# Hymba layer in fp32 on one core: the fold of the second down run, the spread of a row scale, and the Silu table are put elsewhere

## The chip, the cores and the metric

The kernel runs on one core of one Trainium2 chip. The metric is the device time of one execution in microseconds (us). Five engines work side by side: PE (TensorE, matrix products), DVE (VectorE), ACT (ScalarE), POOL (GpSimd) and SP (SyncE, which here only issues DMAs). Each runs its own instructions in order, and they wait for one another by semaphores.

## The reference

One encoder layer, T = 256 tokens, D = 2048, all in fp32. Each sub-layer is normed ahead and behind:

```python
x = x + 0.5 * rms_norm(swiglu(rms_norm(x, pre1), w_gate_up1, w_down1), post1)     # DFF = 5632
h = rms_norm(x, pre_m) @ w_in                                                     # HGRN2 and attention parts
x = x + rms_norm(concat(hgrn2(h), window_attention(h)) @ w_out, post_m)
x = x + 0.5 * rms_norm(swiglu(rms_norm(x, pre2), w_gate_up2, w_down2), post2)
def swiglu(x, w_gate_up, w_down):
    gate, up = split(x @ w_gate_up, 2)
    return (silu(gate) * up) @ w_down
```

The change touches both feed-forward networks (FFN1 and FFN2 below) and one step of the mixer between them.

## The kernel before

**Products.** Every fp32 operand is held as two f32r tiles: `split_act` (L175 to L177) rounds it on ACT (L176, "cast") and forms what is left on DVE (L177, "split"). One product of two such operands is three matmuls, high by high, high by low and low by high (`three`, L441 is the matmul). Weights arrive as `raw` tiles of 1 MB (two blocks of 128 rows by 1024 columns), and a pair of weight blocks is called a pair here.

**Gate and up.** The first stage of a network multiplies the tokens by the gate and up weights in groups of columns. While group 0 runs, the inputs `xt` are not yet normed; the row scale is put to use later. `spread` (L271 to L279) turns the two scale columns into a tile R that has one token's scale in each column: for each half m a tile `dg` is written by DVE as identity times scale (L277), a product with a tile of ones (L278) sums it over the partitions, and DVE copies the PSUM bank to R (L279). `dg` has one buffer, so the second half waits until PE has read the first. It is called in both networks and in the mixer. DVE then multiplies `xt` by R (`even`, L1045). The groups' results go through `units`: Silu of the gate on ACT with the scale as factor (L1075), the product with up on DVE (L1080), transposes on PE (L1100), a copy and a cast on ACT. For group 0 the scale is the norm's own.

**Down.** The second stage, class `Pairs`, goes over the hidden rows in 22 pairs (u = 0 to 21) twice, once for each half of the 2048 columns: the first and the second down run. A plain pair is 8 products (24 matmuls). The even pairs 0 to 18 are mixed pairs and use a scheme of 7 products (21 matmuls) in the manner of Strassen: the left sides are sums of hidden blocks, the right sides sums of weight blocks, and four of the seven go to side sums P1, P5, P6 and P7 that have PSUM banks of their own, beside the four result banks c00, c01, c10, c11. When the last mixed pair is done, `fold` spreads the side sums over the result banks: ACT copies P1 (L528), DVE forms three more sums (L529, L522, L523, L526), then adds one to each result bank (L535 for c00, L539, L543, L545). A result bank takes no product while its add is under way. In the second run, `play` runs the fold ahead of the pair that stands two places behind the last mixed one.

**What sets the order.** The table `orders` in `ffn` gives the pairs of the two runs; `steps` lists them; `added` names the mixed pairs one of whose block sums is formed by an accumulating DMA from POOL (`prepare`, L1234). The body of the runs is written in its order by hand (a manual schedule): at step i it splits pair i+1, prepares i+4, and multiplies pair i. `load_down` issues the next 1 MB load on SP (L1218) as soon as the last split has freed a buffer. The last two pairs of the second run, 20 and 21, are held: `finish` loads them by itself (L152), splits them, and multiplies bank by bank, so that each result bank is complete as early as possible. The splits of `finish` and the fold are put in one order by a scheduler.

Of the kernel before, what the change touches and what calls it, by code (L numbers as in the profile page):

```python
# [11 lines left out]
F32 = mybir.dt.float32  # L12
# [4 lines left out]
AF = mybir.ActivationFunctionType  # L17
# [3 lines left out]
P = 128  # L21
D = 2048
T = 256
# [14 lines left out]
def hymba_layer_kernel(  # L38
# [37 lines left out]
    def nm(s):  # L76
        uid[0] += 1
        return f"{s}_{uid[0]}"
# [76 lines left out]
    def split_load(src, hp=hip, lp=lop, between=None, middle=None):  # L155
        return split(load(src, between), hp, lp, middle)
# [83 lines left out]
    def pre_stats():  # L240
        with tc.issue_after(last["act"].ins):
            pre_stats_now()
# [29 lines left out]
    def spread(factor=rs2):  # L272

        ps = pb()
        for m in range(2):
            dg = stat.tile([P, P], F32, tag="dg", name=nm("dg"), bufs=1)
            nc.vector.tensor_scalar(dg, ident, factor[:, m : m + 1], None, ALU.mult)  # L277
            nc.tensor.matmul(ps[:, m * P : (m + 1) * P], ones, dg, start=True, stop=True)  # L278
        nc.vector.tensor_copy(R, ps[:, :T])  # L279


# [314 lines left out]
    class Pairs(Blocks):  # L596
# [3 lines left out]

        HELD = 2
        firsts = 2

        def __init__(self, w, orders, tiles, sums, room, gain_src, keep=(), near=()):

# [94 lines left out]
        def second_run(self):  # L700
# [3 lines left out]
                    self.gains(m, n)  # L704
            self.run(1)

        def finish(self, mul, post, new_x=None, gain=None, lead=None):


# [1 line left out]
            n_order = len(order)  # L711
            self.post = post
            self.work(n_order - self.HELD)
            held = []
            for u in order[n_order - self.HELD :]:
                held.append((u, *split_load(self.source(u), hp=post, lp=post)))
            close_far()
            self.half_gain(post)
            if new_x:
# [287 lines left out]
    def ffn(gated, w_dn, post_gain, again, gain=None, lead=None, aside=None):  # L1007

        with ExitStack() as st:
# [108 lines left out]
            def some(steps, n):  # L1118
                for _ in range(n):
                    next(steps)  # L1120

            pre_stats()
            last = KT // 2 - 1
            for u in range(gated.pos, KT // 2):
                gated.work(u + 1)
# [56 lines left out]
            def pair_ahead(g, u):  # L1182
# [16 lines left out]
            orders = [  # L1199
                [9, 11, 8, 13, 10, 15, 12, 1, 0, 3, 14, 5, 16, 17, 2, 7, 4, 19, 6, 18, 20, 21],  # L1200

                [2, 7, 4, 9, 6, 11, 8, 13, 10, 12, 15, 0, 5, 14, 3, 16, 1, 18, 17, 19, 20, 21],
            ]
            added = {0: (12, 0, 14, 16, 2, 4, 6, 18), 1: (2, 4, 6, 10, 12, 0, 14, 16, 18)}
            steps = [(r, u) for r in range(2) for u in orders[r]][: 2 * NU - Pairs.HELD]
            in_order = sorted(
                (i - 3.5 if u in added[r] else i, i) for i, (r, u) in enumerate(steps)
            )
# [29 lines left out]
                    )  # L1238

            def splits(i):  # L1240
                if i >= len(steps):
                    return
                r, u = steps[i]
                raw = raws[i]
# [38 lines left out]
            with tc.manual_schedule():  # L1283
# [34 lines left out]
                some(waiting, 1)  # L1318
                some(ahead, 1)
                products(1)  # L1320
                for i in range(2, len(steps)):
                    if i == NU + 18:
                        back_cm.__exit__(None, None, None)
                        early_cm.__exit__(None, None, None)
                        post = rows.post = st.enter_context(post_pool())
                    ahead = splits(i + 1)
                    next(ahead, None)
                    prepare(i + 4)
                    for u in fetch_at.get(i, ()):
                        fetch(u)  # L1330
                    next(ahead, None)
                    products(i)
                    for _ in ahead:
                        pass
                    if i in again_at:
                        sums[again_at[i]] = sums_again(again_at[i])
                    if i == 8:
                        rows.half_gain(far["pool"])
                    if i == NU - 1:
                        rows.second_run()  # L1340
            return rows.finish(
                mul=0.5, post=post, new_x=again, gain=gain and gain(), lead=lead
            )
# [625 lines left out]
```

## Time and profile before

| what | value |
|---|---|
| median of 3 runs | 1833.16 us (1832.65 to 1834.87) |
| the profiled execution | 1832.72 us |
| its span, first to last instruction | 1830.9 us |
| TensorE clock granted, mean | 0.998 |
| PE busy | 99% of the span |
| DVE, ACT, POOL busy | 87%, 62%, 8% |
| DMA | 444.45 MB, 243 GB/s on average |

The profile is of one execution. Its rows give the start in us from the beginning of the span, the duration, the engine, the line of the kernel, the operation, and the tile that is written with those that are read. A bracket at a row's end tells how long the engine stood idle ahead of it and whose result ended that. "x3" is a row of three like instructions with their time in all. Matmuls overlap, so their durations add up to more than the time; the distance between two starts is what one costs.

### The profile page before, as it was taken

What the parts mean: (1) busy time and instruction counts of PE and PEld (TensorE: products, weight loads), DVE (VectorE), ACT (ScalarE), POOL (GpSimd) and SP (SyncE); (2) the same over time, 40 slices, a digit from 0 to 9 for tenths busy, and PEclk for the clock granted to TensorE, in tenths of its full rate; (3) what the DMA queues carried; (4) which work ended last, traced back from release to release, by engine and by line L of the source; (5) the groups of instructions that cost most, each with busy time, mean ns of one, the idle gap of its engine ahead of it and who ended that gap; (6) DMA issues with size and microseconds to landing.
All of it is one profiled execution on the core that took longest, in us unless ns stands there. A gap on an engine that the chain in (4) does not pass through costs nothing.

```text
span 1830.9 us, 23436 instructions
## 1 busy us (share of the span) xinstructions
PE 1812.4 (99%) x8438; PEld 1503.5 (82%) x8438; DVE 1599.2 (87%) x2041; ACT 1130.9 (62%) x1496; POOL 155.5 (8%) x149
## 2 busy tenths in 40 slices
PE   9999999999999999999999999999999999999997
PEld 6888888888888887888888888788888888888886
DVE  7999999999989988477687798899999999998986
ACT  6565666665656666476587556556666666566663
POOL 1011111111011100000000000001111111011110
PEclk9999999999999999999999999999999999999999
DMA  8789999998698985555554456789999888699892
GB/s 301 230 231 289 275 280 255 252 262 242 231 341 267 301 263 192 187 191 165 169 166 150 170 210 245 218 244 266 282 273 270 255 245 253 199 345 290 272 328 106
DMA packets 210420, 444.45 MB, mean 243 GB/s; under 512 B 11656, under 2 KB 46560, under 8 KB 209536
## 3 DMA queue, kind: packets, MB, share of 16 engines
q1 hardware_dynamic: 180032, 385.14, 60.2%
q0 software_dynamic: 30272, 57.82, 18.2%
q8 instruction: 66, 1.08, 0.2%
q14 instruction: 50, 0.41, 0.1%
HBM read 430.31 MB, written 12.60 MB: 242 GB/s over the span
## 4 chain that ended last, share of the span: by engine, by line
PE 89%; DVE 4%; ACT 3%; DMA 2%; issue 2%; POOL 0%; SPq 0%; DVEq 0%; ACTq 0%; POOLq 0%
PE pa L441 39%; PE pb L441 33%; PE pa L309 5%; PE pa L314 3%; PE pa L364 2%; PE pa L363 2%; PE pa L362 2%; DVE l L177 2%; DMA raw<-in_w_ffn_gate_up_dram 2%; ACT h L176 1%; PE pa L1100 1%; PE pb L1100 1%; PE pb L1690 0%; PE pb L1664 0%; PE pb L1768 0%
## 5 line engine op out<-in xcount | busy, mean ns | idle before, releaser
L176 ACT CAST h<-raw 128x1024 fp32r<-128x1024 f32 (+1 forms) x861 | 851.0, 1013 | 467.6 <-PE pb L441 154.5
L177 DVE TENSOR_TENSOR l<-raw,h 128x1024 fp32r<-128x1024 f32 (+1 forms) x861 | 983.8, 1173 | 140.2 <-ACT h L176 106.0
L441 PE MATMUL pa<-h,xt 128*128 128x512 f32 x1104 | 387.9, 392 | 0.1
L441 PE MATMUL pb<-h,xt 128*128 128x512 f32 x952 | 340.7, 392 | 0.5 <-DVE pb L1152 0.4
L441 PEld LDWEIGHTS pa<-h,xt 128*128 128x128 f32 x1104 | 207.2, 188 | 44.2 <-DVE xt L232 0.6
L441 PE MATMUL pa<-l,xt 128*128 128x512 f32 x552 | 216.0, 391 | 0.1
L441 PEld LDWEIGHTS pb<-h,xt 128*128 128x128 f32 x952 | 178.7, 188 | 43.6 <-DVE pb L1159 3.9
L441 PE MATMUL pb<-l,xt 128*128 128x512 f32 x476 | 185.6, 390 | 0.0
L441 PE MATMUL pa<-h,ht 128*128 128x512 f32 x464 | 163.1, 390 | 3.8 <-DVE pa L535 3.8
L441 PE MATMUL pb<-h,ht 128*128 128x512 f32 x464 | 163.0, 390 | 0.0
L936 POOL DMA_DIRECT2D raw<-in_w_ffn_gate_up_dram x76 | 92.0, 1211 | 738.5 <-DVE l L177 647.0
L309 PE MATMUL pa<-xt,h 128*128 128x512 f32 x512 | 124.5, 393 | 0.2 <-ACT h L176 0.2
L441 PEld LDWEIGHTS pa<-l,xt 128*128 128x128 f32 x552 | 103.8, 188 | 21.5 <-DVE l L177 1.7
L309 PEld LDWEIGHTS pa<-xt,h 128*128 128x128 f32 x512 | 93.8, 188 | 18.6 <-ACT h L176 0.6
L441 PE MATMUL pa<-h,xs 128*128 128x512 f32 x304 | 108.9, 389 | 0.0
L441 PE MATMUL pb<-h,xs 128*128 128x512 f32 x304 | 106.0, 389 | 0.0
L441 PEld LDWEIGHTS pa<-h,ht 128*128 128x128 f32 x464 | 87.1, 188 | 22.6 <-issue 4.6
L441 PEld LDWEIGHTS pb<-l,xt 128*128 128x128 f32 x476 | 89.5, 188 | 17.0
L441 PEld LDWEIGHTS pb<-h,ht 128*128 128x128 f32 x464 | 87.1, 188 | 18.0
L441 PE MATMUL pa<-l,ht 128*128 128x512 f32 x232 | 90.4, 390 | 0.0
L441 PE MATMUL pb<-l,ht 128*128 128x512 f32 x232 | 90.3, 389 | 0.0
L1234 POOL DMA_DIRECT2D raw<-in_w_ffn_down_dram x34 | 41.2, 1211 | 366.2 <-DVE la L177 345.9
(287 smaller groups left out, 2550.8 us busy)
## 6 DMA issues: line engine op xcount, KB each, us to landing
raw<-in_w_ffn_gate_up_dram SPq DMA_DIRECT2D x350, 512.0 KB, 5.8
raw<-in_w_ffn_down_dram SPq DMA_DIRECT2D x88, 1024.0 KB, 7.9
raw<-in_w_mix_in_dram SPq DMA_DIRECT2D x52, 1024.0 KB, 4.9
raw<-in_w_ffn_gate_up_dram POOLq DMA_DIRECT2D x76, 512.0 KB, 8.4
raw<-in_w_ffn_down_dram POOLq DMA_DIRECT2D x34, 512.0 KB, 10.1
raw<-in_w_mix_out_dram SPq DMA_DIRECT2D x16, 1024.0 KB, 5.0
ht<-away SPq DMA_DIRECT2D x24, 512.0 KB, 10.5
away<-ht SPq DMA_DIRECT2D x16, 512.0 KB, 6.8
```

The lines of the kernel that those rows point to most:

```text
L176: nc.scalar.copy(hi, src)
L177: nc.vector.tensor_tensor(lo, src, hi.bitcast(F32), ALU.subtract)
L309: nc.tensor.matmul(slot[f], weights(hs, kk, f), xcol(xt, k), start=(k == 0), stop=(k == KT - 1))
L314: nc.tensor.matmul(slot[f][:, 0:T], weights(ls, kk, f), xcol(xt, kh * 8 + kk, 0), start=False, stop=False,)
L362: nc.tensor.matmul(dst, xh, h[:, o : o + n], start=(k == 0), stop=False)
L363: nc.tensor.matmul(dst, xh, l[:, o : o + n], start=False, stop=False)
L364: nc.tensor.matmul(dst, xl, h[:, o : o + n], start=False, stop=(k == KT - 1))
L441: nc.tensor.matmul(self.bank(at), lhs, rhs, start=(n == 1), stop=n in (ends, self.of[at]), skip_group_check=n > ends,)
L936: nc.gpsimd.dma_start(raw[:, 0:1024].rearrange("p (k c) -> p k c", k=2), self.source(u, g)[:, :, 1], accum_op=ALU.add,)
L1100: nc.tensor.transpose(bank[:, o : o + P], zs[m][:, k * P : (k + 1) * P], ident)
L1234: nc.gpsimd.dma_start(raws[i][:, 0:1024].rearrange("p (k c) -> p k c", k=2), Pairs.part(w_dn, u, r)[:, :, 512:1024], accum_op=ALU.add,)
```

## The change

It has three parts.

First, the second run's order is a new one in which mixed and plain pairs alternate strictly to the end; pair 18, mixed, stands at place 18 and pair 19 at place 19 (counted from 0). The held pairs are no longer loaded in `finish`: `steps` covers all 44, so `load_down` loads them in the common row, and `hold` splits them: pair 20 in step NU + 18, ahead of the products of pair 18, and pair 21 in the midst of the fold. The fold is written out behind the last pair of the loop: two parts (the sums and the add to c00), then pair 21's splits, then the other three adds.

Second, `spread` writes both halves of identity times scale into R itself, and one product of 256 columns takes the place of two of 128; the copy back to R stays. The tile `dg` is gone there; the helper `to_columns`, which used the same buffer, has it alone.

Third, behind `pre_stats()` in each network ACT is given one Silu of a 128 by 2 piece of a scratch tile.

The program is written anew around that. DVE at the end of FFN2's second run; `l` are splits (15343 and 15347 of pair 19, 15412 and 15416 of held pair 20, 15422 of held pair 21), `y` the fold's sums, `pa_14643` to `pb_14645` the result banks. Before:

```order
L177 TENSOR_TENSOR l_15343<-raw_10171,h_15342 128x1024
L177 TENSOR_TENSOR l_15412<-raw_15409,h_15411 128x1024
L177 TENSOR_TENSOR l_15347<-raw_10171,h_15346 128x1024
L529 TENSOR_TENSOR y_15374<-pb_14663,y_15374 128x512
L177 TENSOR_TENSOR l_15416<-raw_15409,h_15415 128x1024
L522 TENSOR_TENSOR y_15374<-pb_14664,y_15374 128x512
L177 TENSOR_TENSOR l_15422<-raw_15419,h_15421 128x1024
L523 TENSOR_TENSOR y_15374<-pa_14662,y_15374 128x512
L526 TENSOR_TENSOR y_15374<-pa_14662,y_15374 128x512
L535 TENSOR_TENSOR pa_14643<-pa_14643,y_15374 128x512
L539 TENSOR_TENSOR pa_14644<-pa_14644,y_15374 128x512
L543 TENSOR_TENSOR pb_14645<-pb_14645,y_15374 128x512
```

After (15347 and 15351 are held pair 20's splits, 15407 and 15411 held pair 21's; the result banks are `pa_14634` to `pb_14636`):

```order
L177 TENSOR_TENSOR l_15347<-raw_10162,h_15346 128x1024
L177 TENSOR_TENSOR l_15351<-raw_10162,h_15350 128x1024
L530 TENSOR_TENSOR y_15399<-pb_14654,y_15399 128x512
L523 TENSOR_TENSOR y_15399<-pb_14655,y_15399 128x512
L524 TENSOR_TENSOR y_15399<-pa_14653,y_15399 128x512
L527 TENSOR_TENSOR y_15399<-pa_14653,y_15399 128x512
L536 TENSOR_TENSOR pa_14634<-pa_14634,y_15399 128x512
L177 TENSOR_TENSOR l_15407<-raw_10156,h_15406 128x1024
L177 TENSOR_TENSOR l_15411<-raw_10156,h_15410 128x1024
L540 TENSOR_TENSOR pa_14635<-pa_14635,y_15399 128x512
L544 TENSOR_TENSOR pb_14636<-pb_14636,y_15399 128x512
```

Two splits stood among the fold's sums, and the second split of pair 21 behind all its adds; now the four sums and the first add stand together, the two splits of pair 21 follow, and the other adds come behind those.

DVE at the spread of FFN2: `l` are splits of gate and up weights, `scales` holds the row scale, `xt` the inputs. Before:

```order
L177 TENSOR_TENSOR l_10054<-raw_10046,h_10053 128x1024
L277 TENSOR_SCALAR dg_10027<-ident,scales 128x128
L177 TENSOR_TENSOR l_10096<-raw_10092,h_10095 128x1024
L177 TENSOR_TENSOR l_10100<-raw_10092,h_10099 128x1024
L177 TENSOR_TENSOR l_1837_10187<-raw_10165,h_1836_10186 128x512
L277 TENSOR_SCALAR dg_10030<-ident,scales 128x128
L177 TENSOR_TENSOR l_10133<-raw_10129,h_10132 128x1024
L279 COPY R<-pb_10026 128x256
L1045 TENSOR_TENSOR xt_9624<-xt_9624,R 128x1024 x4
```

After:

```order
L177 TENSOR_TENSOR l_10045<-raw_10037,h_10044 128x1024
L276 TENSOR_SCALAR R<-ident,scales 128x128 x2
L177 TENSOR_TENSOR l_10087<-raw_10083,h_10086 128x1024
L177 TENSOR_TENSOR l_10091<-raw_10083,h_10090 128x1024
L177 TENSOR_TENSOR l_1829_10178<-raw_10156,h_1828_10177 128x512
L280 COPY R<-pb_10020 128x256
L177 TENSOR_TENSOR l_10124<-raw_10120,h_10123 128x1024
L1062 TENSOR_TENSOR xt_9617<-xt_9617,R 128x1024 x4
```

The second half of the scale stood behind three splits; now both are written at the place of the first, and the copy of R stands ahead of the split that it followed. On PE one row, R with ones, 128x256, stands where the first of the two was.

ACT at the first units of FFN2: `h` are casts of weights, `xs` of an input sum, `z` and `s` the Silus of the two halves. Before:

```order
L176 CAST h_10212<-raw_10174 128x1024
L176 CAST h_10216<-raw_10174 128x1024
L176 CAST h_10256<-raw_10165 128x1024
L176 CAST xs_10089<-s_10085 128x4x128
L1075 ACT_TABLE_LOAD
L1075 ACTIVATE z_10180<-pa_9340,scales 128x512
L1075 ACTIVATE s_10182<-pb_9342,scales 128x512
```

After:

```order
L176 CAST h_10203<-raw_10165 128x1024
L176 CAST h_10207<-raw_10165 128x1024
L176 CAST xs_10080<-s_10076 128x4x128
L1092 ACTIVATE z_10171<-pa_9333,scales 128x512
L176 CAST h_10247<-raw_10156 128x1024
L1092 ACTIVATE s_10173<-pb_9335,scales 128x512
```

The table load has left this place; it stands in front of the small Silu, 14 rows earlier, behind the cast of the first split in the rows of DVE above (`h_10044`). The cast that stood ahead of the Silus now stands between them. In FFN1 the small Silu brings no load, since that table is the one in use there.

On SP the gain's load (L661, now L663) stands ahead of the load of held pair 21, where it followed it. In FFN1, POOL's small row loads into the buffer that `dg` shared stand ahead of two small power operations that they followed, and DVE's first split of pair five (there the pair after the spread's) moves behind the scaling of the inputs.

```diff
--- before.py
+++ after.py
@@ -273,9 +273,10 @@
 
         ps = pb()
         for m in range(2):
-            dg = stat.tile([P, P], F32, tag="dg", name=nm("dg"), bufs=1)
-            nc.vector.tensor_scalar(dg, ident, factor[:, m : m + 1], None, ALU.mult)
-            nc.tensor.matmul(ps[:, m * P : (m + 1) * P], ones, dg, start=True, stop=True)
+            nc.vector.tensor_scalar(
+                R[:, m * P : (m + 1) * P], ident, factor[:, m : m + 1], None, ALU.mult
+            )
+        nc.tensor.matmul(ps[:, :T], ones, R, start=True, stop=True)
         nc.vector.tensor_copy(R, ps[:, :T])
 
 
@@ -600,6 +601,7 @@
 
         HELD = 2
         firsts = 2
+        held = None
 
         def __init__(self, w, orders, tiles, sums, room, gain_src, keep=(), near=()):
 
@@ -704,6 +706,21 @@
                     self.gains(m, n)
             self.run(1)
 
+        def hold(self, n, raw=None):
+
+            self.held = self.held or []
+            order = self.orders[1]
+            for _ in range(n):
+                u = order[len(order) - self.HELD + len(self.held)]
+                raw = raw or load(self.source(u))
+                self.held.append((u, *split(raw, hp=self.post, lp=self.post)))
+                raw = None
+
+        def fold_after(self, pos):
+
+            self.after = pos
+            self.rest = 6 * (len(self.order) - pos - 1)
+
         def finish(self, mul, post, new_x=None, gain=None, lead=None):
 
 
@@ -711,9 +728,9 @@
             n_order = len(order)
             self.post = post
             self.work(n_order - self.HELD)
-            held = []
-            for u in order[n_order - self.HELD :]:
-                held.append((u, *split_load(self.source(u), hp=post, lp=post)))
+            if self.held is None:
+                self.hold(self.HELD)
+            held = self.held
             close_far()
             self.half_gain(post)
             if new_x:
@@ -1120,6 +1137,7 @@
                     next(steps)
 
             pre_stats()
+            nc.scalar.activation(warm[:, 0:2], rs2, AF.Silu)
             last = KT // 2 - 1
             for u in range(gated.pos, KT // 2):
                 gated.work(u + 1)
@@ -1199,10 +1217,10 @@
             orders = [
                 [9, 11, 8, 13, 10, 15, 12, 1, 0, 3, 14, 5, 16, 17, 2, 7, 4, 19, 6, 18, 20, 21],
 
-                [2, 7, 4, 9, 6, 11, 8, 13, 10, 12, 15, 0, 5, 14, 3, 16, 1, 18, 17, 19, 20, 21],
+                [2, 7, 4, 9, 6, 11, 8, 13, 10, 15, 12, 5, 0, 3, 14, 1, 16, 17, 18, 19, 20, 21],
             ]
             added = {0: (12, 0, 14, 16, 2, 4, 6, 18), 1: (2, 4, 6, 10, 12, 0, 14, 16, 18)}
-            steps = [(r, u) for r in range(2) for u in orders[r]][: 2 * NU - Pairs.HELD]
+            steps = [(r, u) for r in range(2) for u in orders[r]]
             in_order = sorted(
                 (i - 3.5 if u in added[r] else i, i) for i, (r, u) in enumerate(steps)
             )
@@ -1238,7 +1256,7 @@
                     )
 
             def splits(i):
-                if i >= len(steps):
+                if i >= 2 * NU - Pairs.HELD:
                     return
                 r, u = steps[i]
                 raw = raws[i]
@@ -1318,7 +1336,7 @@
                 some(waiting, 1)
                 some(ahead, 1)
                 products(1)
-                for i in range(2, len(steps)):
+                for i in range(2, 2 * NU - Pairs.HELD):
                     if i == NU + 18:
                         back_cm.__exit__(None, None, None)
                         early_cm.__exit__(None, None, None)
@@ -1329,6 +1347,8 @@
                     for u in fetch_at.get(i, ()):
                         fetch(u)
                     next(ahead, None)
+                    if i == NU + 18:
+                        rows.hold(1, raws[2 * NU - 2])
                     products(i)
                     for _ in ahead:
                         pass
@@ -1338,6 +1358,12 @@
                         rows.half_gain(far["pool"])
                     if i == NU - 1:
                         rows.second_run()
+                        rows.fold_after(NU - Pairs.HELD - 1)
+                fold = rows.fold()
+                some(fold, 2)
+                rows.hold(1, raws[2 * NU - 1])
+                for _ in fold:
+                    pass
             return rows.finish(
                 mul=0.5, post=post, new_x=again, gain=gain and gain(), lead=lead
             )
```

## Prediction

> **What bounds the kernel now.** I read the shares of busy time first, then what the tensor engine waited for, and only then the places of those waits in time. The page's shares of busy time:
>
> ```profile
> PE 1812.4 (99%) x8438; PEld 1503.5 (82%) x8438; DVE 1599.2 (87%) x2041; ACT 1130.9 (62%) x1496; POOL 155.5 (8%) x149
> ```
>
> PE is busy for 99% of the span, so time can come only from fewer products, cheaper products, or the few places where PE stands still. The change keeps the three-product splitting and the number of mixed pairs, so the standing places are what matters. PE's waits (engine and line waited for, total us, times, longest):
>
> ```profile
> PE pa L441 <- DVE pa L535: 3.8, 2, 1.9
> PE pb L278 <- DVE dg L277: 1.1, 1, 1.1
> PE pa L1100 <- DVE s L1080: 0.9, 1, 0.9
> ```
>
> Each of the three belongs to one part of the change: the fold, the spread and the Silu. Together they are 5.8 us, which is the scale of what can be had; the rest is the price of the refilling after a wait and of the removed products.
>
> **Part 1, the fold behind the last pair of the loop.** PE around the fold, FFN1 first and then FFN2 (start, duration, form, idle before in brackets):
>
> ```profile
> 687.35 0.39 PE L441 MATMUL pb<-h,ht 128*128 128x512 f32 x1
> 689.66 0.47 PE L441 MATMUL pa<-h,ht 128*128 128x512 f32 x1 [1.92 <-DVE pa L535]
> ...
> 692.50 0.39 PE L441 MATMUL pb<-h,ht 128*128 128x512 f32 x1
> ```
>
> ```profile
> 1793.44 0.39 PE L441 MATMUL pa<-ha,ht 128*128 128x512 f32 x1
> ...
> 1798.20 0.39 PE L441 MATMUL pa<-h,ht 128*128 128x512 f32 x1
> ...
> 1803.42 0.39 PE L441 MATMUL pb<-h,ht 128*128 128x512 f32 x1
> 1805.73 0.47 PE L441 MATMUL pa<-h,ht 128*128 128x512 f32 x1 [1.92 <-DVE pa L535]
> ...
> 1808.55 0.39 PE L441 MATMUL pb<-h,ht 128*128 128x512 f32 x1
> ```
>
> The mixed pair 18 runs from 1793.44 to 1798.20: 21 matmuls in 4.76, so one costs 0.227, and a plain pair of 24 costs 5.44. From 1803.42 to the next pb bank there are 13 steps, 2.95 at that cadence; they took 5.13, so the stall with its refill costs 2.18. In FFN1 it is 5.15 - 2.95 = 2.20. Why the add is late is in DVE's queue at that place:
>
> ```profile
> 1796.81 3.50 DVE L177 TENSOR_TENSOR l<-raw,h 128x1024 fp32r<-128x1024 f32 x3 [0.81 <-ACT h L176]
> 1800.23 0.69 DVE L529 TENSOR_TENSOR y<-pb,y 128x512 f32<-128x512 f32 x1
> 1800.83 1.22 DVE L177 TENSOR_TENSOR l<-raw,h 128x1024 fp32r<-128x1024 f32 x1
> ...
> 1804.89 0.69 DVE L535 TENSOR_TENSOR pa<-pa,y 128x512 f32<-128x512 f32 x1
> ```
>
> The sums are closed at 1798.2 and the first add on a result bank ends at 1805.6, because splits of pairs 19, 20 and 21 stand ahead of the fold's operations and among them. The result bank is wanted after one plain pair, at 1798.20 + 5.44 = 1803.64.
>
> After the change pair 18 stands one place later and starts at 1793.44 + 5.44 = 1798.88, ends at 1803.64, and pair 19 covers the fold until 1809.08. DVE has the two splits of pair 19 and the two of held pair 20 ahead of the fold (four times about 1.15 by the rows above); with the casts ahead of them I place their end at about 1803.6, an estimate. Then come four fold operations of 0.60 and the add of 0.69: from 1803.8 to 1806.9, wanted at 1809.08, 2.2 us of slack. What is late next is the split of held pair 21, now between the first and the second add: 1806.9 to 1809.3, wanted behind six matmuls at 1810.4 (slack 1.1). The second add then ends at 1809.9, wanted at 1811.8. Its load is one more thing to fit in (the page's DMA issues, with the median us to landing; the second row is for later):
>
> ```profile
> raw<-in_w_ffn_down_dram SPq DMA_DIRECT2D x88, 1024.0 KB, 7.9
> raw<-in_w_ffn_down_dram POOLq DMA_DIRECT2D x34, 512.0 KB, 10.1
> ```
>
> It waits for the last split of pair 18 to free its buffer, which I put at about 1797.7, an estimate (pair 18 starts at 1798.88 and its last split is done by about 1.2 before that). At the median of 7.9, which holds for full DMA engines, it lands at 1805.6, still ahead of 1806.9; a freer queue, as it is there, leaves more room for its cast. The gain load that SP now issues ahead of it waits only for a tile that PE has left by then. Part 1 gives **2.18 + 2.20 = 4.4**. Its cover is the 2.2 us of slack; if DVE comes later than that by the same 2.1 as now, all 4.4 are lost again.
>
> **Part 2, one product for the spread.** PE at the spread of FFN2, of FFN1 (second fence) and of the mixer (third):
>
> ```profile
> 1153.59 0.38 PE L278 MATMUL pb<-dg,ones 128*128 128x128 f32 x2
> 1153.72 0.48 PE L441 MATMUL pa<-h,xt 128*128 128x512 f32 x1
> 1154.05 0.40 PE L441 MATMUL pa<-l,xt 128*128 128x512 f32 x1
> ...
> 1155.99 0.49 PE L278 MATMUL pb<-dg,ones 128*128 128x128 f32 x2 [1.09 <-DVE dg L277]
> ...
> 1156.55 0.40 PE L441 MATMUL pa<-h,xt 128*128 128x512 f32 x1
> ```
>
> ```profile
> 38.55 0.38 PE L278 MATMUL pb<-dg,ones 128*128 128x128 f32 x2
> ...
> 40.16 0.40 PE L441 MATMUL pa<-l,xt 128*128 128x512 f32 x1
> ```
>
> ```profile
> 765.43 0.38 PE L278 MATMUL pb<-dg,ones 128*128 128x128 f32 x2
> ...
> 766.76 0.39 PE L362 MATMUL pa<-h,xt 128*128 128x512 f32 x1
> ```
>
> One spread product that waits for nothing costs 1154.05 - 1153.59 - 0.227 = 0.23. A product with twice the columns is not in this trace: it lies between 0.23 (columns free) and 0.46 (two of them), and I take 0.35, the middle. The pair costs 0.70 in FFN1 (1.61 less four ordinary steps), 0.65 in the mixer (1.33 less three), 1.83 in FFN2 (2.96 less five), where the one-buffer scratch tile makes the second wait. So FFN1 gives **0.35** and the mixer **0.30**. In FFN2 PE itself gains 1.48, but DVE's chain does not:
>
> ```profile
> 1155.05 0.69 DVE L177 TENSOR_TENSOR l<-raw,h 128x512 fp32r<-128x512 f32 x1 [1.67 <-ACT h L176]
> ...
> 1157.59 3.50 DVE L1045 TENSOR_TENSOR xt<-xt,R 128x1024 fp32r<-128x1024 f32 x3
> ...
> 1165.55 1.22 DVE L177 TENSOR_TENSOR l<-raw,h 128x1024 fp32r<-128x1024 f32 x1
> ```
>
> ```profile
> 1167.21 0.39 PE L441 MATMUL pa<-l,xt 128*128 128x512 f32 x1
> ```
>
> Behind the split at 1155.05 now come the copy of R (0.35) and a split of 1.15, so the scaling of the inputs begins at 1157.15 in place of 1157.59: only 0.44 earlier. A later split in that chain, at 1165.55, is read by PE at 1167.21; PE 1.48 early would want it at 1165.73 and get it at 1166.3. So about 0.6 comes back as a wait for that split, and PE arrives at the Silu about 0.8 early. In FFN1 the split of pair five moves behind the scaled inputs on DVE, closer to its use; I count no loss for it, and 0.35 at worst (FFN1's gain).
>
> **Part 3, the Silu table.** ACT's queue ahead of and at the first units of FFN2, and PE's two transposes there:
>
> ```profile
> 1148.34 1.05 ACT L176 CAST h<-raw 128x1024 fp32r<-128x1024 f32 x1 [1.66 <-PE pb L441]
> ...
> 1170.48 3.47 ACT L176 CAST h<-raw 128x512 fp32r<-128x512 f32 x4 [2.85 <-DMA raw<-in_w_ffn_gate_up_dram]
> 1173.85 0.61 ACT L176 CAST xs<-s 128x512 fp32r<-128x512 f32 x1
> 1174.48 1.28 ACT L1075 ACT_TABLE_LOAD   x1
> 1175.78 0.69 ACT L1075 ACTIVATE z<-pa,scales 128x512 f32<-128x512 f32 x1
> ```
>
> ```profile
> 1177.31 0.33 PE L1100 MATMUL pa<-ident,z 128*128 128x128 f32 x1
> 1178.57 0.33 PE L1100 MATMUL pa<-ident,s 128*128 128x128 f32 x1 [0.93 <-DVE s L1080]
> ```
>
> The load of 1.28 goes to the idle 1.66 ahead of the cast at 1148.34. In its place the first cast of the pair behind stands between the two Silus (0.95): xs at 1172.9, Silu z at 1173.5, that cast, Silu s from 1175.2 to 1175.9, the product on DVE to 1176.6, the second transpose at 1176.7 to 1177.0, in place of 1178.57. PE is ready for it at 1176.5. So parts 2 and 3 together move PE in FFN2 by **1.6** (1178.57 less 1177.0); the bounds are 0.8 (PE's lead alone, the wait left) and 1.48 + 0.93 = 2.4. FFN1 needs no load there: its warm-up is one ACT instruction in an idle stretch, at nothing.
>
> [...]
>
> **The sum.** 2.20 + 2.18 + 0.35 + 0.30 + 1.6 = 6.6. The profiled execution took 1832.72 (span 1830.9 and 1.8 around it) and becomes 1826.1; the median of the three runs, 1833.16, lies 0.44 above it, so the forecast is **1826.5**.
>
> **The rivals.** First, **DVE takes back FFN2's lead**. The stretch behind the Silu:
>
> ```profile
> 1177.00:1197.00 20.00, 19.07 (x87) 15.42 (x86) 19.43 (x24) 10.80 (x13) 1.20 (x1) 1.00 0.70 209
> ```
>
> DVE (the third pair of columns) is busy for 19.43 of 20 us, more than PE's 19.07, so a PE that arrives 1.6 early may only wait there for splits. Against it, DVE too starts this stretch earlier. Price 1.6: 1828.1. Second, **the fold's stall stays** at its new place, because DVE ends the held splits 2.2 or more later than I place them: 1826.5 + 4.4 = 1830.9. For it speaks that four splits still stand ahead; against it, that the two of the last held pair and one of pair 19 no longer stand among the fold's operations. Third, on the other side, **loads late in the second down run**. The five plain pairs 15, 5, 3, 1 and 17 each go ahead of the mixed pair before them, so their megabyte is wanted 4.76 sooner, while the DMA engines are full (FFN2's second run; the share is in the column ahead of the last):
>
> ```profile
> 1740.00:1760.00 20.00, 20.00 (x90) 16.57 (x89) 18.45 (x22) 13.44 (x15) 2.43 (x2) 1.00 1.02 333
> ```
>
> If the engines cannot deliver earlier, each run loses 4.76 once, and 2.2 more (10.1 - 7.9) where the accumulating load behind is late too: 7.0 a run, 13.9 in all, 1833.16 + 13.9 - 6.6 = 1840.5. It decides from about 2 us of lateness: pair 15 at place 9 is wanted at about 1750, its load goes out at about 1738 and 7.9 to 10.1 later is 1746 to 1748. Against it, loads are issued in the new order too, so the plain pair's goes out earlier. [...]
>
> **How the numbers follow.** The forecast has 0.55, DVE taking back the lead 0.20, the stall that stays 0.12, late loads 0.08, and 0.05 is for what I have not seen. A measurement of this kernel can tell about 0.2%, 3.7 us, from no change, so faster means below 1829.5. The first two lie there, with a sixth of the third: 0.77. Within 0.2% are the rest of the third, late loads that cost about as much as is gained, and half of the unseen: 0.16. Slower: 0.07. The low end has the Silu and spread at their bounds (0.8 and 0.4 more), and 1.3 for what else may start earlier: 1824.0. The high end takes in the stall that stays: 1831.0.
>
> **What would show it.** In the waits of PE, the row of the fold's first add is gone, or below 0.3, in both networks; if it is there, part 1 failed. The row of the scratch tile is gone, and one product of 256 columns stands at each spread. The wait at the transposes falls from 0.93 to 0.3 or less, with the table load at about 1147. A new wait of PE for a split near 1166 of about 0.6 is expected; one near 51 would show the loss in FFN1. Waits for the down weights in the second run, longer than 1 us, would prove the third rival; a forecast missed by over 1.6 with the fold's row gone would point to the first.

## The result, and the profile after

Six runs of the changed kernel took 1824.65 to 1825.19 us, with a median of **1824.76**; six of the kernel before, the three of the table further up among them, took 1831.67 to 1835.30, with a median of 1833.36. The ratio is 0.9952, with a 95% interval of 0.9939 to 0.9964: faster by 8.6 us, more than the forecast's 6.7 and inside its range. Two things stand out. The spread of the runs fell from 3.6 to 0.5 us. And the profiled executions differ by less than the medians: 1832.72 before, 1824.81 after, 7.9 us.

The waits of PE after the change (engine and line waited for, total us, times, longest), 0.3 us and more, without the rows that stand at nearly the same size in both profiles:

```profile
PE pb L210 <- DMA X<-in_x_dram: 0.8, 1, 0.8
PE pa L442 <- DVE l L177: 0.3, 1, 0.3
```

None of the three rows that the prediction started from is left. The one new row of this size, for a split, is at 11.6 us, and the wait for `X` is for the kernel's input; both are ahead of all that the change touches. Where the 7.9 us came from is seen by laying the two profiles' PE rows beside each other at the same product (start after less start before):

| place on PE | at (before) | shift so far | gained on the way |
|---|---|---|---|
| start of the spread, FFN1 | 38.55 | +0.25 | -0.25 (PE waited longer for the input `X`) |
| transposes of group 0, FFN1 | 63.05 | -0.37 | 0.62, spread and DVE's chain behind it |
| transposes of group 9, FFN1 | 482.96 | -0.43 | 0.06 |
| mixer's first transposes | 705.43 | -2.60 | 2.17, the first fold |
| last transposes ahead of FFN2 | 1127.62 | -2.85 | 0.25, spread of the mixer |
| transposes of group 0, FFN2 | 1178.95 | -5.57 | 2.72, spread and Silu |
| transposes of the last group, FFN2 | 1599.03 | -5.77 | 0.20 |
| last product | 1821.92 | -7.91 | 2.14, the second fold |

DVE at the fold of FFN2 after the change, and PE where the held pairs begin:

```profile
1797.91 0.68 DVE L530 TENSOR_TENSOR y<-pb,y 128x512 f32<-128x512 f32 x1
...
1800.56 0.69 DVE L536 TENSOR_TENSOR pa<-pa,y 128x512 f32<-128x512 f32 x1
1801.15 2.35 DVE L177 TENSOR_TENSOR l<-raw,h 128x1024 fp32r<-128x1024 f32 x2
1803.42 0.69 DVE L540 TENSOR_TENSOR pa<-pa,y 128x512 f32<-128x512 f32 x1
```

```profile
1803.13 0.39 PE L442 MATMUL pb<-h,ht 128*128 128x512 f32 x1
1803.36 0.39 PE L442 MATMUL pa<-h,ht 128*128 128x512 f32 x1
```

The first add ends at 1801.25 and its bank is wanted at 1803.36: 2.1 of slack, where 2.2 were forecast. PE goes from one row to the next in 0.23, with no bracket.

The spread of FFN2 on PE, and DVE behind it:

```profile
1150.73 0.59 PE L279 MATMUL pb<-R,ones 128*128 128x256 f32 x2
1150.98 0.58 PE L442 MATMUL pa<-h,xt 128*128 128x512 f32 x1
1151.39 0.40 PE L442 MATMUL pa<-l,xt 128*128 128x512 f32 x1
```

```profile
1149.30 1.82 DVE L177 TENSOR_TENSOR l<-raw,h 128x1024 fp32r<-128x1024 f32 x2 [1.50 <-ACT h L176]
1151.37 0.43 DVE L280 COPY R<-pb 128x256 f32<-128x256 f32 x1 [0.24 <-PE pb L279]
1152.02 1.23 DVE L177 TENSOR_TENSOR l<-raw,h 128x1024 fp32r<-128x1024 f32 x1 [0.23 <-ACT h L176]
1153.16 4.63 DVE L1062 TENSOR_TENSOR xt<-xt,R 128x1024 fp32r<-128x1024 f32 x4
```

The product costs 1151.39 - 1150.73 - 0.23 = 0.43. The scaling of the inputs starts 2.43 behind the product; it was 1157.59 - 1153.59 = 4.00. ACT and PE at the first units of FFN2:

```profile
1143.85 1.28 ACT L1140 ACT_TABLE_LOAD   x1
...
1168.42 0.62 ACT L176 CAST xs<-s 128x512 fp32r<-128x512 f32 x1
1168.94 0.69 ACT L1092 ACTIVATE z<-pa,scales 128x512 f32<-128x512 f32 x1
1169.53 1.03 ACT L176 CAST h<-raw 128x1024 fp32r<-128x1024 f32 x1
1170.47 0.68 ACT L1092 ACTIVATE s<-pb,scales 128x512 f32<-128x512 f32 x1
```

```profile
1172.94 0.27 PE L1117 MATMUL pa<-ident,z 128*128 128x128 f32 x1
1173.05 0.27 PE L1117 MATMUL pa<-ident,s 128*128 128x128 f32 x1
```

The transposes follow each other in 0.11, where the second had stood 1.26 behind the first.

### The profile page after: what moved, and what is told of

Read it like the earlier page. It is cut to its first block, busy times and chain, and to the rows that moved or that the text cites. A ratio compares the mean times of both kernels' runs of the same rounds, so it can differ in the third digit from the quotient of the medians.

```text
span 1823.0 us, 23428 instructions
## 1 busy us (share of the span) xinstructions
PE 1809.6 (99%) x8432; PEld 1503.0 (82%) x8432; DVE 1599.9 (88%) x2041; ACT 1131.8 (62%) x1498; POOL 155.6 (9%) x149
## 3 DMA queue, kind: packets, MB, share of 16 engines
q8 instruction: 66, 1.08, 0.2%
## 4 chain that ended last, share of the span: by engine, by line
PE 95%; ACT 2%; DVE 2%; DMA 1%; issue 1%; SPq 0%; POOL 0%; DVEq 0%; ACTq 0%; POOLq 0%
PE pa L442 41%; PE pb L442 36%; PE pa L310 5%; PE pa L315 3%; PE pa L365 2%; PE pa L364 2%; PE pa L363 2%; DVE l L177 1%; DMA raw<-in_w_ffn_gate_up_dram 1%; PE pa L1117 1%; PE pb L1117 1%; ACT h L176 0%; PE pb L1716 0%; PE pb L1690 0%; PE pb L1794 0%
```

## The experiments

Two questions were open: which piece of each part does the work, and why the medians moved by more than the profiles. Theory: the parts do what the prediction says. Rival: something that one profiled execution of before did not show stands behind the rest. Times are medians; "before" is the kernel before, run beside it.

**The fold's part alone.**

```diff
 # the changed kernel, with the old spread (two products from dg) and without:
-            nc.scalar.activation(warm[:, 0:2], rs2, AF.Silu)
```

> The first part alone: new order of the second run, held pairs loaded and split in the common row, fold behind pair 19; spread and Silu as before. Theory, the parts add and the fold's is 2.2 in each network: both waits of PE for the fold's first add are gone and the end of the last product moves by 4.3 to 4.5 us against before, nothing else moves; about 1829.0. In FFN2 the wait for the scratch tile (1.1) and the wait at the transposes (0.9) stay. Rival, the new order of the pairs also changes when loads land and so moves other places: over 0.5 us of difference outside the two folds. Second question, the 128x512 weight cast behind the FFN2 spread that before waited 2.27 us for its load and after did not: if the load's landing is chance, the wait may be gone here too; if the spread's new form caused it, it stays.

1828.12 (1827.57 to 1828.66) against 1833.99; ratio 0.9968 (0.9956 to 0.9979). In the trace the folds give 2.22 and 2.14, and both waits are gone. Outside the folds one place moved by more than 0.5 us: the stretch from FFN2's spread to its transposes took 24.56 in place of 25.36, and the next rows say why. Yet the times differ by 5.9: the fold's part is worth more than its two waits. Also, the 128x512 cast ahead of the second scale, which had waited 2.27 for its load, waited 0.45:

```profile
1151.34 0.62 ACT L176 CAST h<-raw 128x512 fp32r<-128x512 f32 x1 [0.45 <-DMA raw<-in_w_ffn_gate_up_dram]
...
1152.36 0.38 PE L278 MATMUL pb<-dg,ones 128*128 128x128 f32 x2
1153.52 0.38 PE L278 MATMUL pb<-dg,ones 128*128 128x128 f32 x2
```

The first row is ACT's, the others PE's. With the old spread PE did not wait for the second scale here. Over all fourteen profiles this cast waited at most 0.91, but for the 2.27 of the one that the prediction was made from. So the wait for the scratch tile, 1.1 us, came with that execution's late load and is no fixture of the old spread: the Silu alone, further down, has the old spread too and does not have this wait. That the load was late by chance is argued, since the kernel before has only this one profile.

**The spread alone.**

```diff
 # the kernel before, with
-            dg = stat.tile([P, P], F32, tag="dg", name=nm("dg"), bufs=1)
-            nc.vector.tensor_scalar(dg, ident, factor[:, m : m + 1], None, ALU.mult)
-            nc.tensor.matmul(ps[:, m * P : (m + 1) * P], ones, dg, start=True, stop=True)
+            nc.vector.tensor_scalar(
+                R[:, m * P : (m + 1) * P], ident, factor[:, m : m + 1], None, ALU.mult
+            )
+        nc.tensor.matmul(ps[:, :T], ones, R, start=True, stop=True)
```

> The second part alone. Theory: 0.27 in FFN1 and 0.22 in the mixer from the dearer second product (one of 256 columns costs 0.43), 0.2 to 0.4 more in FFN1 because DVE's chain starts earlier, and in FFN2 PE gains 1.4 at the spread but waits longer at the transposes, for ACT still loads the table there: 1.3 to 2.0 in place of 0.93, net 0.4 to 1.0. Sum 1.1 to 1.9 us, about 1831.9. Rival, the FFN2 gain stands alone and the wait at the transposes does not grow: 2.2 to 2.7, about 1830.9. The 128x512 cast's wait for its load: gone if the spread's form caused that, there if it was chance or the Silu.

1831.39 (1830.15 to 1832.11) against 1833.99; ratio 0.9985 (0.9976 to 0.9995). The wait at the transposes did not grow, it fell to 0.3: the theory's sentence on ACT fails, since DVE's earlier sums bring ACT's Silus forward as well. The times gained 2.6, which is the rival's 2.2 to 2.7. From the spread's start to the transposes of group 0 FFN2 takes 23.15, against 24.56 in the kernel with the fold alone, whose load came in time too: 1.4. The ten runs fall into two groups, 1830.15 to 1830.99 and 1831.80 to 1832.11, with a mean granted clock of 0.998 in each of the first and 0.997 in each of the second, and the profile shows why. Stretches around the first fold (from:to, length, busy us and count of PE, weight loads, DVE, ACT and POOL, then the granted clock, the DMA share, GB/s):

```profile
687.30:689.60 2.30, 0.38 (x3) 0.05 (x1) 2.30 (x5) 0.23 (x1) 0.00 (x0) 1.00 1.01 330
689.60:691.10 1.50, 1.50 (x5) 1.22 (x6) 1.50 (x3) 1.50 (x2) 0.00 (x0) 0.69 1.04 397
691.10:692.60 1.50, 1.50 (x5) 1.16 (x4) 1.50 (x3) 0.26 (x1) 0.00 (x0) 0.50 0.39 149
692.60:694.10 1.50, 1.50 (x6) 1.18 (x5) 1.50 (x2) 0.00 (x0) 0.00 (x0) 0.68 0.45 37
694.10:695.60 1.50, 1.50 (x8) 1.22 (x7) 0.53 (x1) 0.00 (x0) 0.00 (x0) 1.00 0.92 341
```

Behind the wait the clock is granted at 0.50 for about 3.4 us, and PE starts 5 or 6 matmuls in 1.5 us in place of 8. In the profile of the kernel before the clock stays at 1.00 behind the same wait (rows from 685.26 on, under "Waits made on purpose"). The stage lost 1.64 us more than in the profile of before. The second fold of this execution was not followed by it.

**The Silu alone.**

```diff
 # the kernel before, with
             pre_stats()
+            nc.scalar.activation(warm[:, 0:2], rs2, AF.Silu)
```

> The third part alone. Theory: the wait of 0.93 at the transposes goes, nearly whole, 0.7 to 1.2 us in FFN2 and nothing in FFN1: about 1832.3. Rival, the wait was hidden behind the chain of DVE and the load of 1.28 only moves it: 0.3 or less. The wait of PE for the scratch tile (1.1) stays.

1833.41 (1832.63 to 1834.81) against 1833.99; ratio 1.0001 (0.9992 to 1.0011): no difference that the times can show, where 1832.3 was expected; runs that the low clock spreads over 2.2 us hide a gain of 1.0. In the trace the stretch from the spread to the transposes takes 23.55, 1.0 less than with the fold alone; 0.6 of the wait is left, and a cast stands between the Silus. The wait for the scratch tile, which was expected to stay, is not there. Here both folds' waits, again 1.92, were followed by the low clock, at 1.60 and 1.57 us.

**The change without the Silu.** The edit takes out the `warm` line alone.

> The change without its third part. Theory, parts two and three overlap in FFN2: the wait at the transposes is back and longer than the 0.93 of before, 1.2 to 2.0, because PE comes 1.4 us earlier from the spread while the table load still stands there; 1.2 to 2.0 slower than the whole change, about 1826.4. Rival, ACT moves along with PE and the table load costs what it did before: 0.9 slower, 1825.7.

1826.33 (1826.08 to 1826.68), 1.57 above the whole change, though the two were not run beside each other. PE, second transpose, and ACT's load in its old place:

```profile
1169.58 1.28 ACT L1092 ACT_TABLE_LOAD   x1
1170.87 0.69 ACT L1092 ACTIVATE z<-pa,scales 128x512 f32<-128x512 f32 x1
```

```profile
1173.65 0.33 PE L1117 MATMUL pa<-ident,s 128*128 128x128 f32 x1 [0.38 <-DVE s L1097]
```

Only 0.4 is waited here, but DVE and PE stay behind, and at the next group's transposes the trace is 1.2 later than the whole change's. So the time came out as the theory had it, but not its reason: the loss is 0.4 of waiting and the rest in the products that follow, which no row shown here explains. The overlap of the two parts is there. Parts two and three take 1.4 and 1.0 alone and 1.9 (24.56 - 22.65) together.

**The pairs in the old order.** Fold and held pairs stay as changed.

```diff
-                [2, 7, 4, 9, 6, 11, 8, 13, 10, 15, 12, 5, 0, 3, 14, 1, 16, 17, 18, 19, 20, 21],
+                [2, 7, 4, 9, 6, 11, 8, 13, 10, 12, 15, 0, 5, 14, 3, 16, 1, 18, 17, 19, 20, 21],
```

> The whole change, but the second run's pairs in the order of before (18 at place 17, 17 at place 18); fold and held pairs stay where the change puts them. Theory, the gain comes from where the fold and the held splits stand, and the order only sets how much room the fold has: DVE is free to begin the fold 5.4 earlier, no wait at the first add, the same time as the change within 0.5 us. Rival, the alternation keeps loads and DVE in step: waits of PE for splits or for the first add of 1 us or more, 1826 or more.

1824.84 (1824.57 to 1825.33): the same as the change. DVE begins the fold 2.3 earlier, not 5.4, and its first add even waits for PE to finish the bank's products:

```profile
1795.60 0.69 DVE L530 TENSOR_TENSOR y<-pb,y 128x512 f32<-128x512 f32 x1
...
1799.26 0.70 DVE L536 TENSOR_TENSOR pa<-pa,y 128x512 f32<-128x512 f32 x1 [0.93 <-PE pa L442]
```

**The held pairs left to `finish`.**

```diff
-            steps = [(r, u) for r in range(2) for u in orders[r]]
+            steps = [(r, u) for r in range(2) for u in orders[r]][: 2 * NU - Pairs.HELD]
...
-                    if i == NU + 18:
-                        rows.hold(1, raws[2 * NU - 2])
...
-                some(fold, 2)
-                rows.hold(1, raws[2 * NU - 1])
```

> The whole change, but the two held pairs are loaded and split in finish, in the order that the scheduler chooses, as before; new order, fold behind pair 19, spread and Silu as changed. In FFN2's order of DVE one split of the last held pair then stands among the fold's sums (1.15 of a slack of 2.1) and its other split behind the third add (about 0.8 before PE reads it). Theory, it is the fold's place behind pair 19 that takes the wait away, and the placing of the held splits by hand is not needed: no wait for the first add, within 0.5 of the change, 1824.8 to 1825.2. Rival, without it the first add or the last split is late by 1 us or more in one or both networks: 1826 to 1828.

1825.08 (1824.83 to 1825.44), with no wait of PE for the fold or for a split of these pairs. So neither the order nor the placing by hand is needed while the other stays. What both runs and the change have in common, and the kernels with the wait have not, is that the fold stands behind pair 19; that this alone pays is concluded from that, for no run here takes out order and placing together or moves the fold back alone.

**Two products, no scratch tile.**

```diff
-            nc.vector.tensor_scalar(
-                R[:, m * P : (m + 1) * P], ident, factor[:, m : m + 1], None, ALU.mult
-            )
-        nc.tensor.matmul(ps[:, :T], ones, R, start=True, stop=True)
+            half = R[:, m * P : (m + 1) * P]
+            nc.vector.tensor_scalar(half, ident, factor[:, m : m + 1], None, ALU.mult)
+            nc.tensor.matmul(ps[:, m * P : (m + 1) * P], ones, half, start=True, stop=True)
```

> The whole change, but the spread keeps two products of 128 columns, read from the two halves of R; the scratch tile is still gone. Theory, the one product saves little and the early second half is what counts: each spread costs 0.5 to 0.7 instead of 0.43, no wait for the scale on PE, 0.3 to 0.8 slower in all, 1825.3. Rival, with the second scale ready early the two products run back to back and cost no more than one: no difference within 0.2.

1824.70 (1824.54 to 1825.10): the rival held.

```profile
1151.10 0.60 PE L278 MATMUL pb<-R,ones 128*128 128x128 f32 x4
1151.46 0.48 PE L441 MATMUL pa<-h,xt 128*128 128x512 f32 x1
1151.78 0.39 PE L441 MATMUL pa<-l,xt 128*128 128x512 f32 x1
```

Back to back, two products cost 1151.78 - 1151.10 - 0.23 = 0.45, against 0.43 for the one. With other products between them the two cost 0.70 (FFN1) and 0.65 (mixer) in the kernel before.

**The last pair's splits behind all adds.**

```diff
-                fold = rows.fold()
-                some(fold, 2)
+                for _ in rows.fold():
+                    pass
                 rows.hold(1, raws[2 * NU - 1])
-                for _ in fold:
-                    pass
```

> The whole change, but the last held pair's splits stand behind all four adds of the fold. In the changed kernel they end 1.2 before PE reads the first; three adds of 0.6 ahead of them make that 0.6 late: a wait of PE for a split of 0.6 in each network, 1.2 to 1.6 slower, 1826.2, and no lower clock from so short a wait. Rival, PE does not come to that split so soon, and the time does not change.

1827.37 (1826.98 to 1827.74), 2.6 above the change and 1.2 above what was expected. PE waits for both splits in each network, 0.61 and 0.17, then 0.33 and 0.16; the loss in the trace is 1.35 and 1.02, where one wait of 0.6 a network was planned. A slack of 1.2 was there and the order of the four adds spends it.

**Waits made on purpose.** To learn when the clock falls, both splits of the last pair go ahead of the fold, and the very last is repeated (none, one, two, four times), which delays the first add.

```diff
+                rows.hold(1, raws[2 * NU - 1])
+                u, hs, ls = rows.held[-1]
+                for _ in range(1):
+                    nc.vector.tensor_tensor(
+                        ls[1], raws[2 * NU - 1][:, 1024:2048], hs[1].bitcast(F32), ALU.subtract
+                    )
                 fold = rows.fold()
                 some(fold, 2)
-                rows.hold(1, raws[2 * NU - 1])
                 for _ in fold:
                     pass
```

> The whole change, but the last held pair's two splits are put ahead of the fold instead of behind its first add. They push the first add by 2.3 us against a slack of 2.1 seen in the changed kernel, so PE waits about 0.2 in each network: 0.3 to 0.6 slower than the change, about 1825.2. Rival, DVE is not what the first add waits for (the casts or the last load are) and then nothing changes or the last split is late by 1 us or more: 2 us slower.

> As the kernel with both held pairs ahead of the fold, with the very last split done once more on DVE (same values), so that the first add comes another 1.15 later: a wait of PE of 1.3 to 1.4 in each network. Theory, a wait costs its own length, and one as short as this does not lower the granted clock: 2.7 to 2.9 slower than the change, 1827.6, runs close together. Rival, any wait of over a microsecond may be followed by some 3.3 us at a clock of 0.50, which costs 1.6 more: runs in groups 1.6 apart, up to 1830.8.

> The same with the last split done three times in all: a wait of 2.4 to 2.5 in each network, a little more than the 1.92 of the kernel before. Theory, a wait of about 2 us lets the clock drop to 0.50 for some 3.3 us in a part of the executions, at 1.6 each: runs in groups at about 1830.0, 1831.6 and 1833.2, with half or more of the waits followed by the lower clock. Rival, the low clock of two earlier profiles behind the fold was chance with no tie to the wait: all runs at about 1830.0.

> The same with the last split done five times in all: a wait of 4.7 to 4.8 in each network. Theory, so long a wait is always followed by the low clock: 2 x (4.75 + 1.6) slower than the change, 1837.5, runs close together again. Rival, the low clock comes in a part of the executions whatever the length: groups from 1834.3 to 1837.5.

The medians are 1827.36, 1832.22, 1835.83 and 1842.82, all above what was expected. One reason is that in FFN1 the scheduler put splits of the mixer's weights among the fold's rows and made those waits longer (1.60, 3.63, 4.78 and 7.36). In FFN2 they are near the plan (0.16, 1.40, 2.67 and 5.24). The other is the low clock, which lasted 6.8 us and not 3.4 behind the three longest: against the change the fold with the wait of 7.36 lost 9.74, the one with 5.24 lost 8.24. PE where the held pairs begin, with one, two and four repeats (FFN1, FFN2):

```profile
696.79 0.76 PE L442 MATMUL pa<-h,ht 128*128 128x512 f32 x1 [3.63 <-DVE pa L536]
...
1810.80 0.47 PE L442 MATMUL pa<-h,ht 128*128 128x512 f32 x1 [1.40 <-DVE pa L536]
```

```profile
697.87 0.77 PE L442 MATMUL pa<-h,ht 128*128 128x512 f32 x1 [4.78 <-DVE pa L536]
...
1813.89 0.47 PE L442 MATMUL pa<-h,ht 128*128 128x512 f32 x1 [2.67 <-DVE pa L536]
```

```profile
700.33 0.77 PE L442 MATMUL pa<-h,ht 128*128 128x512 f32 x1 [7.36 <-DVE pa L536]
...
1818.67 0.76 PE L442 MATMUL pa<-h,ht 128*128 128x512 f32 x1 [5.24 <-DVE pa L536]
```

The first product took 0.76 or 0.77 behind the four waits that the low clock followed, and 0.47 behind the two where the clock stayed at 1.00, as behind both folds of the kernel before (0.47 at 1.00). With the kernels that have the fold's old place:

| idle time of PE ahead of the first add (us) | followed by the low clock |
|---|---|
| 0.16, 1.40, 1.60 | in none of 3 |
| 1.92 (profiles of before, of the spread alone, of the Silu alone) | in 3 of 6 |
| 2.67 | not in this one |
| 3.63, 4.78, 5.24, 7.36 | in all 4 |

The runs with four repeats lie close together again (1842.35 to 1843.02), as expected where every wait ends in the low clock; those with one and two are spread over 2.3. The rival of the third kernel, that the low clock has no tie to the wait, falls.

Which wait is hit can be read from the clock's own steps. In each of the fourteen profiles they lie a whole multiple of 3.413 us apart (before, full clock for 1819.304, which is 533 times 3.413; after, for 1812.477, 531 times; with the spread alone, full for 682.666, 200 times, low for 3.413, full again for 1129.812, 331 times), so in these profiles the clock changed only at the edges of a grid of that step. These are stretches of that grid around folds (columns as above), of the kernel before, of the spread alone (second fold) and of the Silu alone (second fold):

```profile
685.26:688.67 3.41, 2.48 (x11) 1.71 (x10) 3.41 (x5) 0.68 (x1) 0.00 (x0) 1.00 0.98 332
688.67:692.08 3.41, 2.42 (x11) 2.01 (x12) 3.41 (x6) 2.00 (x2) 0.00 (x0) 1.00 0.75 282
692.08:695.50 3.42, 3.42 (x17) 2.84 (x16) 2.62 (x3) 0.00 (x0) 0.00 (x0) 1.00 0.55 170
```

```profile
1802.91:1806.32 3.41, 1.54 (x7) 1.31 (x8) 3.41 (x6) 0.00 (x0) 0.00 (x0) 1.00 0.00 0
1806.32:1809.73 3.41, 3.41 (x17) 2.82 (x16) 1.23 (x2) 0.00 (x0) 0.00 (x0) 1.00 0.02 5
```

```profile
1803.48:1806.90 3.42, 1.50 (x7) 0.95 (x6) 3.42 (x7) 0.00 (x0) 0.00 (x0) 1.00 0.00 0
1806.90:1810.31 3.41, 3.41 (x10) 2.65 (x9) 1.69 (x2) 0.00 (x0) 0.00 (x0) 0.50 0.02 5
```

In the kernel before, the wait of 1.92 lay across an edge at both folds, so that no stretch was idle for more than 1.03, and the clock stayed. In the three cases that were hit it lay whole in one stretch. In the case that was not hit with the spread alone, 0.05 of it lay ahead of the edge and 1.87 behind. The waits made on purpose agree: the most idle time in one stretch was 1.40, 1.55, 1.60 or 1.78 where full clock followed, and 3.09 to 3.41 where the low clock followed. So do the other stretches from the first full clock on: up to the last product PE was idle for at most 1.09 us of one in the profile of before and 1.08 in that of after, and the clock stayed at 1.00; behind the last product, with 3.00 and 2.74 us idle in a stretch, it was 0.50. Over all fourteen profiles the least idle time of a stretch that 0.50 followed is 1.92, and the most that 1.00 followed is 1.87. The 1.87 is one case, and both figures rest on ends of matmuls that the profile models. Behind the folds the low clock lasted 3.4 us where PE was idle for at most 0.39 of the first halved stretch, and 6.8 where it was idle for 0.94 or more of it (the waits of 4.78, 5.24 and 7.36), and the mean granted clocks of the three executions, 0.998 with one, 0.997 with two and 0.995 with four repeats, go with that; what ends the low clock was not tested further.

## Why the prediction was right, and where it was not

**The fold: right in mechanism and size, but a term was left out.** 2.17 and 2.14 against 2.20 and 2.18, with slacks of 2.1 and 1.2 against 2.2 and 1.1, and no load late. The step that failed is the refill: "the stall with its refill costs 2.18" was read from an execution in which neither wait was followed by the low clock. In the three cases where it was, it cost 1.57 to 1.64 more. The 63 runs of the kernel before, beside the change and all these kernels, have a median of 1834.0, 1.3 above the profiled one, which is about 0.8 of such an event per run, an estimate. The grid gives nearly the same, an estimate too: if it lies anywhere against the program, a wait of 1.92 falls whole into a stretch of 3.41 in (3.41 - 1.92) / 3.41 = 0.44 of the cases, and two waits make 0.9 per run. This also is why the spread of the runs shrank: without a wait there is nothing to hit. The runs of before beside the experiments show it: 16 with a mean clock of 0.999 took 1832.17 to 1833.29, five with 0.996 took 1835.44 to 1836.44; all six of the change have 0.998 or 0.999.

**The spread: right in sign, wrong in reason.** The 256-column product cost 0.43, not 0.35, and so FFN1 and the mixer gave 0.27 and 0.22 on PE. The number of products made little difference here (0.45 for two back to back). FFN1 gave another 0.35, where splits that had come just in time came earlier (before, one ended at 59.93 and PE read it at 59.99); the prediction feared the contrary there.

**FFN2: 2.7 in place of 1.6.** The step "about 0.6 comes back as a wait for that split" failed: no wait near 1166, since the scaling of the inputs began 1.6 earlier relative to PE, not 0.44. That step took the late load at 1154.39 for given, and with it the 128x512 split in front of the copy of R. In the other thirteen profiles the cast waits at most 0.91 for that load. With the load in time parts two and three are worth 1.9. The rest of the 2.7 is that one execution's wait. So the sizes of 7.9 and 8.6 are in part chance: the profiles' gain holds about 0.8 of one late load, and the medians' holds low clock, which the sum of 6.6 left out.

**The Silu: right.** The transposes no longer wait; taking the line out costs 1.2 in the trace and 1.6 in the times. The load itself takes no more than its 1.28 in the rows of the change without the Silu: 0.01 lies between its end at 1170.86 and the Silu at 1170.87.

**The rivals.** DVE did not take back FFN2's lead (shift -5.57 at group 0, -5.77 at the last). The stall did not stay, and the loads did not come late: the median landing of the down weights is 7.8 against 7.9.

## What to carry to other kernels

Price a stall of TensorE with what may follow it: here a wait of 1.9 us cost 2.2 and, in the three of six cases in which it lay whole in one stretch of the clock's grid, 1.6 more of lowered clock, while waits of 1.6 and less were not followed by it. A kernel whose run times are spread by steps of that size may have such a wait: here the spread fell from 3.6 to 0.5 us when the two were gone. A wait that one profile shows may be that execution's late load: look at it in a second profile before you count on its going. When a change has several pieces, take them out one by one: here the new order, the placing by hand and the wider product could each go without loss.

## What the runs showed of the hardware that was not expected

In the fourteen profiles the clock of TensorE changed only at the edges of a grid of 3.41 us. Behind a stretch with 1.92 us of idle PE it was 0.50 for the next one, while it stayed at 1.00 where the same wait lay across an edge and left at most 1.03 us (or, once, 1.87) idle in one stretch. A product of fp32 tiles of 128x128 costs little by itself: two of them back to back take 0.45 and one of 256 columns 0.43, but two with f32r products between them take 0.65 to 0.70. And one 512 KB load came later in one execution than in all others, though these are of kernels that differ: the cast behind it waited 2.27 there, and 0 to 0.91 in the other thirteen.
